# Low parts of three groups of weights made by VectorE in place of GpSimd, in a two-layer hybrid decoder

## The chip, the cores and the metric

The kernel runs on one core of a Trainium2 chip. The metric is the device time of one execution in microseconds (us), where less is better. The engines are named as in the profile: PE is TensorE's matmul stream and PEld its weight loads, DVE is VectorE, ACT is ScalarE, POOL is GpSimd, SP is SyncE, whose queue issues the kernel's DMA transfers.

## The reference

Two post-norm layers over x of 512 positions and 1024 features, all in float32. Each layer has a token mixer with three kinds of heads that read one combined projection of x, an output projection, a layer norm, a SwiGLU FFN of width 2816 and a second layer norm.

```python
proj = x @ w_in                                   # 1024 -> A 1152, B 768, C 416 columns
o_a = dilated_mixture(q, k, v, bias)              # A: 6 heads of 64, three (window, dilation) pairs
o_b = diff_attention(q1, q2, k1, k2, v, lam)      # B: 4 heads, two softmax maps each
o_b = rms_norm(o_b, subln_g) * (1 - lam_init)
c_q, c_kv, k_r = split(c_in, [256, 384])          # C: latents of 256 and 128, rotary key of 32
q  = rms_norm(c_q,  q_norm_g)  @ w_uq             # up-projection of the queries, 256 -> 6 x 96
kv = rms_norm(c_kv, kv_norm_g) @ w_ukv            # up-projection of keys and values, 128 -> 6 x 128
o_c = causal_attention(q_with_rope, k_with_rope, kv_values)
heads = concat([o_a, o_b, o_c])                   # 16 heads x 64 = 1024
h = layer_norm(ALPHA * x + heads @ w_o, ln1)      # output projection, 1024 x 1024
x = layer_norm(ALPHA * h + (silu(h @ w_gate) * (h @ w_up)) @ w_down, ln2)
```

## The kernel before

**Products in three parts.** Every float32 operand of a projection is split in two: a high part, which ACT writes as a rounded copy, and a low part, the operand minus its high part. A product is three matmuls (`mm3`, lines 210 to 212): high by high, high by low, low by high. So each chunk of weights goes through `split` (lines 199 to 205): ACT makes `whi` (line 201), and another engine makes `wlo` (line 202) from `raw` and `whi`, both in the core's own memory (SBUF).

**Chunks of weights.** `prep_one` brings one chunk of 128 rows and up to 1024 columns: SP issues the load into `raw` (two buffers, line 147), and `split` fills a pair of `whi` and `wlo` (five buffers of each). Chunks follow a fixed order over the whole kernel, and a step that needs some calls `chunks`, which prepares up to five ahead. Their names: `wva`, `wa` (A's values; queries and keys), `wvb`, `wb` (B's), `wc` (C's latents), `wu` (C's up-projections, three chunks of 768 columns a layer), `woa` and `wo` (output projection: four chunks of 768 columns for A's heads, five of 1024 for B's and C's), `wgu` and `wd` (FFN).

**Who makes the low part.** A table `ENG` names the engine for each group: "g" for GpSimd, "v" for VectorE. The norm factors of C (`q_norm_g`, `kv_norm_g`, in the tile `small`) are folded into the rows of `wu`. With GpSimd they are multiplied into `raw` by DVE first (line 159), and then the chunk is split like any other; with VectorE there is another path:

```python
        if scale is not None and eng is gp:
            v.tensor_scalar(raw[:, :w], raw[:, :w], scale, None, op0=ALU.mult)
            scale = None
        split(hi[:, :w], lo[:, :w], raw[:, :w], scale, eng)
...
            sc.activation(hi, src, AF.Copy, scale=scale)
            v.scalar_tensor_tensor(lo, src, scale, hi.bitcast(F32), op0=ALU.mult, op1=ALU.subtract)
```

**Steps of a layer's mixer.** `STEPS` lists them: values and queries of A and B, heads `AH`, `BH`, C's latents `CI`, their transposes `CT` (line 623, split into `x` by line 202), C's values `CV`, heads `CH`, norms of B `BN`, and shares of the output projection `W0` to `W5`, each of which adds a block of `heads @ w_o` into the residual (line 427) and gives PE work between the heads. `WC` is the rest of the output projection with the first layer norm. A softmax block (`softmax_block`) goes from PE's logits to DVE (line 289: bias and maximum; line 292: reciprocal), ACT (line 291: exponential) and POOL (line 299, for A and C: division by the sum). B's heads combine two maps: POOL scales one (line 566) and DVE adds the other (line 567). The maps are then transposed by PE (line 314), split into `pt` and `pu` by ACT and DVE, and multiplied by the values (line 536). C's queries are multiplied with the rotary table by DVE (line 656) and their low part is made by POOL (line 202, `qk<-m,qk`). `norm_b` spreads B's norm factors with a copy on DVE (line 582) and applies them (line 586).

**Order.** Each engine works through its own queue in the order in which the program was compiled. That order is set by a planner, which takes the ready instruction of the highest priority by a timeline with estimated costs; `PRIO` shifts single steps in it. So a change of the engine of an instruction can also change the order around it. SP's queue issues the loads of weights in line with the copies that stack queries and keys (line 525).

Of the kernel before, what the change touches and what calls it, by code (L numbers as in the profile page):

```python
# [49 lines left out]

ACTS = "qk qk m m qk qk m qk qk hd m hd qk hd qk qk e4 qk qk e4 qk qk".split()

ENG = {"wva": "g", "wa": "g", "wvb": "v", "wb": "g", "wc": "v", "wu": "g", "woa": "g", "wo": "g", "wgu0": "v",
       "wgu1": "v", "hA": "v", "hB": "g", "hC": "g", "qC": "g", "latq": "s", "latkv": "s"}

EARLY = 4
# [11 lines left out]
def hybrid_decoder(ctx: ExitStack, tc: tile.TileContext, I, out):  # L68
# [13 lines left out]
    def on(key):  # L82
        return {"v": v, "g": gp, "s": sc}[ENG.get(key, "v")]

# [865 lines left out]
```

## Time and profile before

| | us |
|---|---|
| median of 3 runs (lowest, highest) | 1212.33 (1210.52, 1213.17) |
| profiled execution, its own time | 1210.01 |
| its span, first to last instruction | 1208.2 |
| PE busy in the span | 1174.8 |
| DVE busy | 835.0 |
| ACT busy | 657.5 |
| POOL busy | 290.6 |

Busy times overlap, since the engines run side by side. An engine can be busy for longer than its instruction needs: a row's duration includes time in which the instruction had been started and waited for a port or a clock. Idle time of PE is what the other engines can still give back.

### The profile page before, as it was taken

To read this page: it belongs to the slowest core of one execution; us is meant where nothing else is said; L and a number is where in the kernel's file an instruction comes from. 1 tells how busy PE (TensorE), PEld (TensorE's weight loads), DVE (VectorE), ACT (ScalarE), POOL (GpSimd) and SP (SyncE) were. 2 spreads that over 40 slices of the span, in tenths; PEclk is the share of its full clock that TensorE was granted. 3 is DMA by queue.
4 is the path that set the end of the run, shared out by engine and by line. 5 is a ranking of instruction groups with operands and counts; after the bars stand their busy time and mean duration, and the time that the engine had idled before them with its cause. 6 is when DMAs were issued, how large, how long until landed. Compare 5 with 4: busy or idle time off the path is not lost.

```text
span 1208.2 us, 20278 instructions
## 1 busy us (share of the span) xinstructions
PE 1174.8 (97%) x7582; PEld 1073.2 (89%) x7582; DVE 835.0 (69%) x1655; ACT 657.5 (54%) x1290; POOL 290.6 (24%) x307
## 2 busy tenths in 40 slices
PE   9999999989999999999989999899999999999997
PEld 8889888889999999888888999787899999998885
DVE  5267788798888887443562677987988888864435
ACT  5466667666555555332443666775655565543322
POOL 1542576430000000000363435873200000000003
PEclk9999999999999999999999999999999999999999
DMA  7784321322333334333228544231123333344321
GB/s 263 201 243 136 116 75 46 97 69 88 106 106 105 102 99 136 119 114 95 80 88 232 149 131 124 82 106 35 55 91 108 110 105 94 105 140 132 96 70 70
DMA packets 50838, 136.41 MB, mean 113 GB/s; under 512 B 7731, under 2 KB 9267, under 8 KB 50739
## 3 DMA queue, kind: packets, MB, share of 16 engines
q1 hardware_dynamic: 50736, 135.10, 36.6%
q8 instruction: 60, 0.98, 0.3%
q14 instruction: 42, 0.32, 0.1%
HBM read 115.15 MB, written 2.10 MB: 97 GB/s over the span
## 4 chain that ended last, share of the span: by engine, by line
PE 55%; issue 29%; DVE 8%; ACT 3%; POOL 2%; DMA 2%; SPq 0%; POOLq 0%; ACTq 0%; DVEq 0%
PE psacc L210 10%; PE psacc L211 9%; PE psacc L212 9%; PE pss L210 4%; PE pss L212 4%; PE pss L211 4%; PE pspv L536 3%; PE pstp L314 2%; PE pss L286 2%; PE pstp L210 2%; PE pstp L211 2%; PE pstp L212 2%; DVE res L371 1%; POOL st L365 1%; DMA raw<-in_wva 1%
## 5 line engine op out<-in xcount | busy, mean ns | idle before, releaser
L201 ACT ACTIVATE whi<-raw 128x1024 fp32r<-128x1024 f32 (+2 forms) x150 | 153.4, 1025 | 130.0 <-PE pstp L212 26.2
L202 POOL TENSOR_TENSOR wlo<-raw,whi 128x1024 fp32r<-128x1024 f32 (+1 forms) x44 | 98.3, 2243 | 380.6 <-ACT whi L201 380.6
L202 DVE TENSOR_TENSOR wlo<-raw,whi 128x1024 fp32r<-128x1024 f32 (+1 forms) x106 | 129.1, 1221 | 47.8 <-ACT whi L201 47.7
L210 PE MATMUL psacc<-x,whi 128*128 128x256 f32 (+1 forms) x446 | 146.1, 333 | 2.3 <-ACT x L201 2.1
L202 DVE TENSOR_TENSOR wlo<-w,whi 128x1024 fp32r<-128x1024 f32 (+1 forms) x120 | 123.8, 1044 | 34.4 <-ACT whi L201 34.2
L211 PE MATMUL psacc<-x,whi 128*128 128x256 f32 (+1 forms) x446 | 147.0, 332 | 0.0
L212 PE MATMUL psacc<-x,wlo 128*128 128x256 f32 (+1 forms) x446 | 146.6, 331 | 0.0
L291 ACT ACTIVATE e<-e,sm 128x128 f32<-128x128 f32 (+3 forms) x160 | 89.4, 559 | 54.2 <-DVE sm L289 52.5
L201 ACT ACTIVATE whi<-w 128x1024 fp32r<-128x1024 f32 (+1 forms) x120 | 107.7, 909 | 6.3 <-DVE w L183 2.1
L210 PE MATMUL psacc<-whi,hd 128*128 128x512 f32 (+1 forms) x296 | 108.0, 367 | 2.0 <-DVE x L202 2.0
L211 PE MATMUL psacc<-wlo,hd 128*128 128x512 f32 (+1 forms) x296 | 106.6, 360 | 0.0
L212 PE MATMUL psacc<-whi,hd 128*128 128x512 f32 (+1 forms) x296 | 103.7, 360 | 0.0
L365 POOL TENSOR_TENSOR st<-st,mhalf 128x1 f32<-128x1 f32 x15 | 14.8, 988 | 349.6 <-DVE st L364 349.6
L210 PEld LDWEIGHTS psacc<-x,whi 128*128 128x128 f32 x446 | 84.0, 190 | 9.9 <-ACT x L201 2.6
L211 PEld LDWEIGHTS psacc<-x,whi 128*128 128x128 f32 x446 | 84.8, 190 | 7.3 <-DVE x L202 0.7
L210 PE MATMUL pss<-x,whi 128*128 128x256 f32 x320 | 91.2, 285 | 0.0
L212 PEld LDWEIGHTS psacc<-x,wlo 128*128 128x128 f32 x446 | 84.8, 190 | 6.9
L212 PE MATMUL pss<-x,wlo 128*128 128x256 f32 x320 | 90.6, 283 | 0.0
L212 PE MATMUL pss<-S,wlo 128*128 128x256 f32 x320 | 90.6, 283 | 0.0
L210 PE MATMUL pss<-S,whi 128*128 128x256 f32 x320 | 90.5, 283 | 0.0
L211 PE MATMUL pss<-S,whi 128*128 128x256 f32 x320 | 90.5, 283 | 0.0
L211 PE MATMUL pss<-x,whi 128*128 128x256 f32 x320 | 90.5, 283 | 0.0
(267 smaller groups left out, 3396.6 us busy)
## 6 DMA issues: line engine op xcount, KB each, us to landing
raw<-in_wgu SPq DMA_DIRECT2D x48, 512.0 KB, 3.6
raw<-in_wd SPq DMA_DIRECT2D x44, 512.0 KB, 3.5
w<-in_wgu SPq DMA_DIRECT2D x40, 512.0 KB, 4.4
qk<-qk SPq DMA_DIRECT2D x72, 128.0 KB, 4.5
qk<-qk SPq DMA_DIRECT2D x128, 64.0 KB, 2.0
raw<-in_wa SPq DMA_DIRECT2D x12, 512.0 KB, 3.6
bias<-in_bias SPq DMA_DIRECT2D x20, 256.0 KB, 4.4
raw<-in_wo SPq DMA_DIRECT2D x10, 512.0 KB, 3.6
```

The costliest lines, as they stand in the source:

```text
L201: sc.activation(hi, src, AF.Copy)
L202: eng.tensor_tensor(lo, src, hi.bitcast(F32), op=ALU.subtract)
L210: pe.matmul(o, ah, bh, start=first, stop=False, skip_group_check=parts)
L211: pe.matmul(o, ah, bl, start=False, stop=False, skip_group_check=parts)
L212: pe.matmul(o, al, bh, start=False, stop=last, skip_group_check=parts)
L286: pe.matmul(s[:, :w], q[:, i * P:(i + 1) * P], kn[:, :w], start=n == 0, stop=n == len(k) - 1)
L291: sc.activation(e, e, AF.Exp, bias=m, scale=-1.0, accum_out=den)
L314: pe.transpose(b[:, c:c + P], es[i][:, j * P:(j + 1) * P], ident)
L365: gp.tensor_tensor(rstd, var, mhalf[:, 0:1], op=ALU.pow)
L371: v.scalar_tensor_tensor(c, c, rstd, b[0], op0=ALU.mult, op1=ALU.add)
L536: pe.matmul(acc[:, j * P:], va, part, start=j + n == 0, stop=j + n == NTB)
```

## The change

Three entries of `ENG` change: the low parts of `wu`, `woa` and `wo` are made by VectorE. For `wu` this also takes the other path of `prep_one` and `split`: the multiplication of `raw` by the factors (line 159) is not issued, ACT multiplies while it writes the high part, and DVE makes the low part as `raw * factor - whi` in one instruction.

```diff
-ENG = {"wva": "g", "wa": "g", "wvb": "v", "wb": "g", "wc": "v", "wu": "g", "woa": "g", "wo": "g", "wgu0": "v",
+ENG = {"wva": "g", "wa": "g", "wvb": "v", "wb": "g", "wc": "v", "wu": "v", "woa": "v", "wo": "v", "wgu0": "v",
        "wgu1": "v", "hA": "v", "hB": "g", "hC": "g", "qC": "g", "latq": "s", "latkv": "s"}
```

## Rows read from the trace of the kernel before

**Rows 1.** The page, part 1: busy time, share of the span, instructions.

```profile
PE 1174.8 (97%) x7582; PEld 1073.2 (89%) x7582; DVE 835.0 (69%) x1655; ACT 657.5 (54%) x1290; POOL 290.6 (24%) x307
```

**Rows 2.** Windows: length, then busy PE, PEld, DVE, ACT, POOL, then PEclk, DMA.

```profile
140.00:232.00 92.00, 86.43 (x520) 76.03 (x519) 76.91 (x214) 65.50 (x152) 58.48 (x61) 0.94 0.29 89
750.00:832.00 82.00, 76.87 (x469) 66.34 (x469) 71.30 (x193) 61.64 (x142) 56.00 (x56) 1.00 0.27 84
```

**Rows 3.** Waits of PE in 140 to 232: total us, times, longest.

```profile
PE psacc L210 <- DVE x L202: 2.0, 1, 2.0
PE pstp L314 <- DVE e L567: 1.7, 1, 1.7
PE pss L286 <- DVE sm L289: 0.9, 1, 0.9
```

**Rows 4.** Waits of PE in 750 to 832.

```profile
PE pstp L314 <- DVE e L567: 2.1, 2, 1.2
PE pss L210 <- DVE sm L289: 1.0, 1, 1.0
```

**Rows 5.** Chain of work, 140 to 155: start, us, what.

```profile
141.02 3.57 DMA raw<-in_wu
...
144.62 0.62 DVE raw L159
...
146.38 2.04 DVE raw L159
...
149.07 0.58 PE psacc L210
```

**Rows 6.** Timeline of POOL, 136 to 150: start, us, instruction.

```profile
146.20 1.81 POOL L202 TENSOR_TENSOR wlo<-raw,whi 128x768 fp32r<-128x768 f32 x1 [0.15 <-ACT whi L201]
```

**Rows 7.** Windows, after two waits of PE and between them, columns alike.

```profile
147.90:154.70 6.80, 5.63 (x25) 5.53 (x26) 5.08 (x14) 3.77 (x7) 4.55 (x6) 0.50 0.33 116
155.00:161.80 6.80, 6.80 (x54) 6.77 (x54) 5.70 (x23) 5.09 (x13) 4.86 (x4) 1.00 0.52 145
182.00:185.40 3.40, 3.40 (x16) 3.10 (x14) 1.96 (x7) 2.99 (x8) 2.22 (x4) 0.50 0.31 122
```

**Rows 8.** Timeline, 177 to 185, two engines.

```profile
178.05 2.37 POOL L202 TENSOR_TENSOR wlo<-raw,whi 128x1024 fp32r<-128x1024 f32 x1
178.12 2.85 DVE L567 SCALAR_TENSOR_TENSOR e<-e,sm,e 128x512 f32<-128x512 f32 x1
```

**Rows 9.** Timeline of DVE, 752 to 800.

```profile
756.62 2.30 DVE L567 SCALAR_TENSOR_TENSOR e<-e,sm,e 128x512 f32<-128x512 f32 x1
...
774.25 0.43 DVE L582 COPY hd<-st 128x512 f32<-128x512 f32 x1
...
793.36 2.47 DVE L582 COPY hd<-st 128x512 f32<-128x512 f32 x1
```

**Rows 10.** Timeline of POOL, 750 to 806.

```profile
756.56 4.05 POOL L202 TENSOR_TENSOR wlo<-raw,whi 128x768 fp32r<-128x768 f32 x2
...
793.14 4.91 POOL L202 TENSOR_TENSOR wlo<-raw,whi 128x1024 fp32r<-128x1024 f32 x2
```

**Rows 11.** Groups of POOL by form: busy us, mean ns, idle before.

```profile
L202 POOL TENSOR_TENSOR wlo<-raw,whi 128x1024 fp32r<-128x1024 f32 x28 | 68.0, 2437 | 50.6 <-ACT whi L201 50.5
L202 POOL TENSOR_TENSOR wlo<-raw,whi 128x768 fp32r<-128x768 f32 x16 | 30.3, 1903 | 330.1 <-ACT whi L201 330.1
```

**Rows 12.** Groups of DVE by form.

```profile
L202 DVE TENSOR_TENSOR wlo<-raw,whi 128x832 fp32r<-128x832 f32 x8 | 8.2, 1025 | 1.3 <-ACT whi L201 1.3
...
L159 DVE TENSOR_SCALAR raw<-raw,small 128x768 f32<-128x768 f32 x6 | 5.3, 888 | 1.2 <-DMA raw<-in_wu 1.2
...
L586 DVE SCALAR_TENSOR_TENSOR hd<-hd,subg,pspv 128x512 f32<-128x512 f32 x4 | 3.0, 742 | 0.0
```

**Rows 13.** Line 202 on DVE, weights: ns min/median/max, first and last start.

```profile
L202 DVE TENSOR_TENSOR wlo<-raw,whi x106: 1007/1220/1898, 16.2 to 1174.3; 128x1024 fp32r<-128x1024 f32 x98, 128x832 fp32r<-128x832 f32 x8
```

**Rows 14.** Queue of SP, 118 to 160: issues merged.

```profile
132.21 8.69 SPq L525 DMA_DIRECT2D qk<-qk  x12
```

## Prediction

> **What bounds the kernel now.** I read the page first: PE is busy for 1174.8 of 1208.2 us [rows 1], so only some 33 us can be won by feeding it better. Then the waits of PE by stretch, to see whom it waits for. Wherever the three moved groups of weights are prepared, which is the second half of the mixer in each layer (about 140 to 232 us and 750 to 832 us), PE's releaser is DVE [rows 3, 4], through short instructions of the softmax, the splits and the combination of B's maps. These two stretches are the ones to study: PE is idle in them for 92.0 - 86.4 = 5.6 and 82.0 - 76.9 = 5.1 us, DVE is busy 84% and 87% of the time, POOL 64% and 68% [rows 2]. DVE is thus second in line, and at first sight the change gives it more to do. The next view speaks for the change: the timelines of DVE and POOL side by side. DVE's long instructions there are not long by nature. The combination of B's maps took 2.85 us at 178.12, beginning 0.07 us after a low part on POOL (178.05 to 180.42), and ended 0.55 us after it [rows 8]; an instruction of the same shape and operands takes 0.74 [rows 12]. The same happens at 756.62, 2.30 us beside two low parts [rows 9, 10]; the copy of B's norm factors takes 2.47 us beside two low parts and 0.43 elsewhere [rows 9, 10]; and the multiplication of C's factors took 2.04 us on the chain at 146.38, beside the low part that POOL had begun at 146.20, where the one before took 0.62 [rows 5, 6]. So a low part on POOL holds DVE up, and PE stands behind: 2.0 us at 149.07 [rows 3, 5], 1.7 us behind line 567 [rows 3], 1.2 us of the 2.1 in layer 2 [rows 4]. After the two longest waits PE also ran at half clock: PEclk is 0.50 (the 1.2 GHz level) from 147.9 to 154.7 and from 182.0 to 185.4, and 1.00 (2.4 GHz) between [rows 7].
>
> **What the change removes.** 24 instructions on POOL. Six low parts of wu and eight of woa at 1.90 us, and ten of wo at 2.44 [rows 11]: 14 x 1.90 + 10 x 2.44 = 51 us of POOL's 290.6 [rows 1]. It also removes six multiplications on DVE, 5.3 us with their stalls [rows 12].
>
> **What it adds.** 24 instructions on DVE. A low part of 1024 columns takes 1.22 us [rows 13], one of 832 columns 1.025 [rows 12], so one of 768 about 1.025 - 64 x (1.22 - 1.025) / 192 = 0.96. For wu the instruction also takes a factor for each row; the nearest row is the 512-column one of line 586, 0.742 us [rows 12], and at 1.025 / 832 = 1.23 ns a column, 768 come to 0.742 + 256 x 0.00123 = 1.06, with the 0.96 of the plain form as lower end. I take 1.0. In all 6 x 1.0 + 8 x 0.96 + 10 x 1.22 = 25.9 us, against 5.3 removed, and without the stalls seen above (2.11 + 1.56 of line 567, 2.04 of line 582): net about +15 us of DVE. The factors cost ACT nothing that I can bound above zero: it writes the same high parts, with a scale in the same instruction.
>
> **What a later order does to queues.** No load is added or moved in SP's list, but a raw buffer is now given back by DVE instead of POOL. In layer 1 the load of wu was issued at 141.02 and took 3.57 us to land [rows 5], because twelve copies of queries and keys occupied SP from 132.2 to 140.9 [rows 14]. If that stays, ACT must make the high part after the landing (it took about 1 us: from the end of the multiplication, 145.24, to the start of POOL's low part, 146.20 [rows 5, 6]), and the new instruction, if it stands at the head of DVE's queue, holds back from 144.6 to 145.6 and then works until 146.6, with the logits of B's head and the split of C's latents (line 202, `x`) behind it. A second chunk behind it would end near 147.6, and the split could begin there instead of at 148.42, the end of the second multiplication [rows 5]. So this place gains between 0.8 us (head of the queue) and 2.9 us (0.9 + 2.0 [rows 3], when it is elsewhere). I take 2.5, since the shorter occupation of the buffers lets the load go earlier.
>
> **The sum.** Gains on PE's side, if the stalls go:
> - 2.5 us at 145 to 149, as above, and the half clock behind it. There PE made 25 matmuls in 5.63 us (0.225 each) against 54 in 6.80 (0.126) at full clock [rows 7]; at that pace 25 would take 3.15, an estimate that neglects the mix of sizes: 2.5 us.
> - 1.7 us at 181 [rows 3], and 16 matmuls in 3.40 us [rows 7], which would take 2.0: 1.4 us.
> - in layer 2 1.2 us behind line 567, and 1.0 behind line 289 [rows 4], which came right after the stalled copy: 2.2 us.
>
> Together 10.3 us, at most about 10.7. Against this stands DVE. Taking those low parts that fell within the two stretches: layer 1 gets two of wu, two of woa and five of wo, 2.0 + 1.9 + 6.1 = 10.0 us, and loses 0.62 + 2.04 of multiplications and 2.11 of the stall: +5.2. Layer 2 gets two, one and five, 2.0 + 1.0 + 6.1 = 9.1 us, and loses 0.6, 1.56 and 2.04: +4.9. Together +10.1 us. DVE now idles there for 15.1 and 10.7 us [rows 2], 25.8 in all; if the stretches shrink by the whole 10.3, 15.5 are left, and the addition takes 10.1 / 15.5 = 0.65 of them. Nothing in the rows says which share of new work falls on the path that PE waits for. Its lower end is zero (all of it slips into idle time), its upper end all of it; I take the share of idle time that it uses up, 0.65, so 6.6 us are given back. Net: 10.3 - 6.6 = 3.7 us, and from the profiled 1210.0 this makes 1206.3. The median of the runs lies 2.3 us above the profiled execution, so I forecast 1208.5. Outside the two stretches, the first chunks of woa (two or three of 0.96 us in each layer) find DVE with room, and the FFN is untouched.
>
> **A rule against it.** A low part on DVE reads two operands in SBUF, and of 106 such low parts the longest took 1.90 us instead of 1.22 [rows 13]: they can be held up by POOL too, by up to 0.68. POOL after the change is busy in the two stretches for about 58.5 - 19.8 = 38.7 and 56.0 - 17.9 = 38.1 us, 42% and 46%; 17 low parts x 0.44 x 0.68 = 5.1 us of DVE at most, 3.3 on the path at the share above. The Trainium skill (SBUF — State Buffer, Who interferes with whom) states that a VectorE instruction with two inputs in SBUF and a GpSimd instruction that reads SBUF exclude each other for their whole length, whichever starts first going first. The stalls at 178.12 and 756.62 agree with it, in size too (2.85 us against the 2.37 of the low part). By that rule the new low parts would also hold up POOL's normalisations, so the change would exchange one exclusion for another.
>
> **Rivals.**
> - *DVE becomes the bound (slower).* Place: the heads of C in both layers, where low parts of 1.22 us stand in DVE's queue in front of the maxima (line 289), reciprocals and splits. For it: DVE is 84% and 87% busy already, and every wait of PE ends on it [rows 2 to 4]. Against it: POOL's queue gets shorter by 20 and 18 us, and POOL stands in the same softmax chains. Price: the gains of 10.3 are replaced by waits of the same length, and 0.65 of 10.1 us comes on top: 1212.3 + 6.6 = 1219; with half the gains kept, 1214. It decides once DVE would have to be over about 91% busy: (76.9 + 5.2 + 71.3 + 4.9) / 174 = 91% at the present lengths. The added work alone brings it there, which is why I take this rival seriously.
> - *The exclusion turns round (no change).* The 3.3 us above eat the net gain of 3.7: 1208.5 + 3.3 = 1211.8.
> - *All the gain stays.* The new work fits into DVE's idle time: 1212.3 - 10.3 = 1202.0, at best 1201.6.
>
> **Chances.** Net gain as summed, or more of it, 0.48 (of this, all the gain 0.10); the exclusion turned round or another balance within 0.2%, 0.21; DVE the bound, 0.31. About 0.2% (2.4 us) is what a measurement of this kernel can tell from no change. The likeliest alone has 1202 to 1210. The range for 8 in 10 goes from 1201, all gains, to 1217, between the two prices of the slower rival.
>
> **What the profile after would show.** Right: line 159 is gone; line 202 has 20 instructions on POOL under `wlo`; lines 567 and 582 have no duration above 2 us beside a low part (beside `qk<-m,qk` some of 1.5 remain); PEclk stays at 1.00 from 147 to 185; POOL is busy for about 240 us, DVE for about 850; PE's waits in the two stretches sum to under 6 us. Wrong: waits of PE that end on lines 289, 202 or 567 of DVE with a low part of `wu`, `woa` or `wo` just before them in DVE's queue; DVE above 93% in the stretches; low parts on DVE of 1.6 us and more; a new half-clock stretch after such a wait. A planner's order that differs in steps far from the change (queries, B's heads) would also make it wrong; the trace before cannot tell of that.

## The result: half a per cent slower, and the profile after

| us | before | after |
|---|---|---|
| median of 9 runs each (lowest, highest) | 1211.82 (1209.46, 1213.17) | 1218.65 (1212.66, 1219.90) |
| ratio, 95% interval | | 1.0053 [1.0039, 1.0067] |
| profiled execution, its span | 1210.01, 1208.2 | 1219.52, 1217.7 |

The change costs about 6.4 us by the ratio. The forecast was 1208.5, faster by 3.7 us; the range ended at 1217.

Busy times of the whole span, part 1 of the page, beside [rows 1]:

```profile
PE 1181.4 (97%) x7582; PEld 1078.4 (89%) x7582; DVE 845.8 (69%) x1673; ACT 658.4 (54%) x1290; POOL 245.6 (20%) x283
```

POOL lost 45 us and 24 instructions, DVE gained 10.8 us. The two stretches, beside [rows 2]:

```profile
140.00:232.00 92.00, 87.08 (x538) 76.45 (x537) 82.12 (x230) 65.56 (x157) 42.50 (x53) 0.98 0.30 92
750.00:832.00 82.00, 76.94 (x461) 68.04 (x461) 74.77 (x197) 58.45 (x135) 34.63 (x43) 0.96 0.29 96
```

DVE went from 84% to 89% and from 87% to 91%; that it was not more is the point to which the experiments come back. Line 159 is gone, and what was moved costs what was forecast (groups of DVE by form, then of POOL, beside [rows 11, 12]):

```profile
L567 DVE SCALAR_TENSOR_TENSOR e<-e,sm,e 128x512 f32<-128x512 f32 x8 | 8.3, 1035 | 1.3 <-POOL e L566 1.3
...
L202 DVE TENSOR_TENSOR wlo<-raw,whi 128x768 fp32r<-128x768 f32 x8 | 7.9, 990 | 0.4 <-ACT whi L201 0.3
...
L205 DVE SCALAR_TENSOR_TENSOR wlo<-raw,small,whi 128x768 fp32r<-128x768 f32 x6 | 6.1, 1014 | 0.8 <-ACT whi L204 0.8
```

```profile
L202 POOL TENSOR_TENSOR wlo<-raw,whi 128x1024 fp32r<-128x1024 f32 x18 | 43.4, 2421 | 47.7 <-ACT whi L201 47.6
...
L202 POOL TENSOR_TENSOR wlo<-raw,whi 128x768 fp32r<-128x768 f32 x2 | 3.7, 1845 | 320.6 <-ACT whi L201 320.6
```

PE's waits in 140 to 232, beside [rows 3], and then in 750 to 832, beside [rows 4]:

```profile
PE pstp L314 <- DVE e L567: 2.5, 1, 2.5
PE pstp L314 <- DVE pu L202: 0.6, 1, 0.6
```

```profile
PE pss L210 <- DVE sm L289: 1.8, 2, 1.5
PE psacc L210 <- DVE x L202: 1.1, 1, 1.1
PE pstp L314 <- DVE e L567: 0.8, 1, 0.8
PE pspv L536 <- DVE hd L586: 0.7, 1, 0.7
```

The wait of 2.0 us on the split of C's latents is gone in layer 1, as forecast. The wait behind line 567 has grown from 1.7 to 2.5, though line 567 is no longer held up for 2.85 us by a low part of POOL. In layer 2 the waits have become more. PE's idle time in the two windows is still 4.9 and 5.1 us.

Two timelines show the new exclusions. First DVE (two rows) and POOL (one row) at 178:

```profile
178.62 1.24 DVE L202 TENSOR_TENSOR wlo<-raw,whi 128x1024 fp32r<-128x1024 f32 x1
180.46 1.74 DVE L567 SCALAR_TENSOR_TENSOR e<-e,sm,e 128x512 f32<-128x512 f32 x1 [0.59 <-POOL e L566]
...
178.62 1.81 POOL L566 TENSOR_SCALAR e<-e,sm,neglam 128x512 f32<-128x512 f32 x1 [0.60 <-DVE sm L292]
```

The low part, now on DVE, and POOL's scaling of B's second map begin together; the low part takes its usual 1.24 us, the scaling 1.81 where the same shape took 0.77 at 782.40 in this run. Line 567, which needs it, waits 0.59 us, and PE behind it. Then at 785, DVE and POOL:

```profile
785.39 1.82 DVE L202 TENSOR_TENSOR wlo<-raw,whi 128x1024 fp32r<-128x1024 f32 x1
...
783.14 2.99 POOL L202 TENSOR_TENSOR qk<-m,qk 128x512 fp32r<-128x512 f32 x2
```

Here POOL was first, and the low part took 1.82 us. The Trainium skill (SBUF — State Buffer, Who interferes with whom) says that the one that starts first goes first and the other stands for its whole length; the case at 785 agrees in kind, with 0.6 us added to the low part.

One part of the profiled difference comes before the first moved instruction. Up to 113 us the queues of both kernels are alike, yet this execution was 4.1 us late at 98 us, behind a wait for a copy of queries into place (timeline of PE):

```profile
83.66 0.58 PE L210 MATMUL psacc<-whi,x 128*128 128x256 f32 x1 [3.65 <-DVE qk L205]
```

In the profile of before this wait was 0.2 us; in other executions of the same two kernels it was 1.58 us (before, again) and 2.02 us (after, again). So the profiles are compared below by stretch, and the verdicts rest on medians.

### The profile page after: what moved, and what is told of

Its sections match the earlier page's. It is cut to its first block, busy times and chain, and to the rows that moved or that the text cites. A ratio compares the mean times of both kernels' runs of the same rounds, so it can differ in the third digit from the quotient of the medians.

```text
span 1217.7 us, 20264 instructions
## 1 busy us (share of the span) xinstructions
PE 1181.4 (97%) x7582; PEld 1078.4 (89%) x7582; DVE 845.8 (69%) x1673; ACT 658.4 (54%) x1290; POOL 245.6 (20%) x283
## 4 chain that ended last, share of the span: by engine, by line
PE 54%; issue 29%; DVE 9%; DMA 3%; POOL 2%; ACT 2%; POOLq 0%; ACTq 0%; DVEq 0%
PE psacc L210 9%; PE psacc L211 9%; PE psacc L212 9%; PE pss L210 4%; PE pss L212 4%; PE pss L211 4%; PE pspv L536 3%; PE pstp L314 2%; PE pstp L210 2%; PE pss L286 2%; PE pstp L211 2%; PE pstp L212 2%; DVE wlo L202 1%; DVE res L371 1%; DMA qk<-qk 1%
## 5 line engine op out<-in xcount | busy, mean ns | idle before, releaser
L201 ACT ACTIVATE whi<-raw 128x1024 fp32r<-128x1024 f32 (+2 forms) x144 | 148.4, 1032 | 128.0 <-PE pstp L212 27.3
L202 DVE TENSOR_TENSOR wlo<-raw,whi 128x1024 fp32r<-128x1024 f32 (+2 forms) x124 | 150.1, 1213 | 47.4 <-ACT whi L201 47.2
L202 POOL TENSOR_TENSOR wlo<-raw,whi 128x1024 fp32r<-128x1024 f32 (+1 forms) x20 | 47.1, 2363 | 368.2 <-ACT whi L201 368.2
L289 DVE CUSTOM_DVE_ANT_0 e<-pss,bias 128x128 f32<-128x128 f32 (+3 forms) x160 | 76.1, 476 | 15.9 <-PE pss L286 12.2
```

The source lines that it names most:

```text
L201: sc.activation(hi, src, AF.Copy)
L202: eng.tensor_tensor(lo, src, hi.bitcast(F32), op=ALU.subtract)
L289: v.tensor_tensor_reduce(out=e, in0=s[:, :w], in1=bias[:, S - w:], op0=ALU.add, op1=ALU.min, scale=-1.0, scalar=-NEG, accum_out=m)
```

## The experiments

Theories, under the letters of the texts on record where they have one there. **L (load):** in the second halves of the mixers, what DVE is given comes out on PE's path nearly whole. **P (planned order):** moving 24 instructions makes the planner lay out the work anew, and the loss is in that layout. **C (chain):** only the wait for the low part itself, or the exclusion of two readers, costs; work that nobody waits for does not. At first also **A**, that the low parts of `wu` gain and those of the output projection lose, and its rival **O**, that any change of an engine disturbs the order by as much. In the first two texts C and D mean something else: that the early wait near 83 us belongs to the changed program (C), or comes and goes with the execution (D). Ratios are to before on the same chip, with 95% intervals.

**1 and 2. Both kernels again** (no edit).

> The kernel before, unchanged, timed and profiled once more. Up to about 115 us the queues of all engines are alike in the kernels before and after, yet the profile of after has a wait of PE of 3.6 us near 83 us that the profile of before has not (0.2 us there, 1.7 us a little later). Theory D (that wait is a matter of when the copies of queries and keys land, and comes and goes from one execution to the next): ratio 1.000, and single times spread over some 4 us; the wait near 83 us can be there or not. Theory C (it belongs to the changed program): no wait above 2 us near 83 us here.

> The changed kernel, unchanged, timed and profiled once more. Theory C (the wait near 83 us belongs to the changed program): the wait of 3 to 4 us is there again, and the ratio stays at 1.005 to 1.006. Theory D: it may be gone, and then the span is some 4 us shorter, about 1213.5; the ratio over many runs then holds a mean of both. In both, the waits of the second half of layer 2 stay: about 5 us are lost between 740 and 835 us.

Measured: before 0.9991 [0.9974, 1.0008]; after 1216.84 us, 1.0048 [1.0031, 1.0065]. The loss is confirmed, and D held: the wait near 83 us was 1.58 and 2.02 us here, and between the same matmuls of layer 2 (740 to 832 us) the second profile of the change lost 4.2 us. The second profile of before held a surprise. Both long waits of layer 1 are there again:

```profile
PE psacc L210 <- DVE x L202: 2.0, 1, 2.0
PE pstp L314 <- DVE e L567: 1.7, 1, 1.7
```

but the clock behind them is full (windows from each wait on, PEclk after the counts; compare the 0.50 in [rows 7]):

```profile
149.00:152.40 3.40, 3.40 (x29) 3.36 (x30) 3.40 (x11) 2.44 (x7) 3.25 (x3) 1.00 0.37 115
181.00:184.40 3.40, 3.40 (x28) 3.21 (x27) 3.20 (x8) 2.38 (x7) 1.88 (x2) 1.00 0.06 20
```

So the half clock behind these two waits was a matter of that execution, and two terms of the sum rested on it.

**3 and 4. One half of the change each.**

```diff
-       "wu": "g", "woa": "g", "wo": "g"
+       "wu": "v", "woa": "g", "wo": "g"      # 3
+       "wu": "g", "woa": "v", "wo": "v"      # 4
```

> Only the low parts of C's up-projection go to VectorE (with the factors in the same instruction); woa and wo stay on GpSimd. Theory A (the loss comes from low parts of woa and wo in VectorE's queue between the heads of C, while wu alone removes the multiplication that a low part on GpSimd held up): a gain of 3 to 5 us near 145 to 155 us in layer 1 stays, nothing is lost behind it, ratio 0.996 to 0.999. Rival O (any change of an engine disturbs the planned order by as much): a loss of 2 us or more, ratio above 1.002.

> Only the low parts of the output projection (woa and wo, 18 chunks) go to VectorE; wu stays on GpSimd with its multiplication on VectorE. Theory A: all of the loss and more, 5 to 9 us, ratio 1.004 to 1.008, since the gain near 150 us is not there. Rival O: between 0.999 and 1.004, with no relation to the parts.

Measured: `wu` alone 1.0044 [1.0027, 1.0060], `woa` and `wo` alone 1.0076 [1.0052, 1.0100]. Theory A fell with the first of the two (0.996 to 0.999 expected), O with the second (0.999 to 1.004). And the halves come to 1.2% together, the whole to 0.5%: something other than these instructions differs among the kernels, and that can be their order.

**5. The change in layer 1 alone.**

```diff
         eng = on(...)
+        if name in ("wu", "woa", "wo") and l == 0:
+            eng = v
```

> The change in layer 1 alone; layer 2 keeps GpSimd's low parts. Theory L: layer 1's second half as in the change (0 to 3 us later than before by 237 us), layer 2's second half as in before (0, within 1.5 us), together 1.001 to 1.003 (1212 to 1215). Theory P: the planner's layout of layer 2 differs as well, so layer 2 need not be as in before: its second half comes out anywhere from 2 us earlier to 10 us later although none of its instructions has changed, and the total 1.000 to 1.008.

Measured: 1.0017 [1.0001, 1.0033], inside the forecast of L. Layer 2's second half ran as in before, with the same waits (1.29 and 0.82 us behind 567, 0.98 behind 289). So most of the loss belongs to layer 2.

**6 to 8. Engines and order taken apart.** The kernel is traced twice in one program. The first trace, with one choice of engines, is planned; its order is then imposed on the second, with another choice, by edges that bind the issue order of each engine and are not meant to add a wait. The six multiplications of line 159, which only one of the two traces has, are left to the planner.

```python
for n in ranks:                       # the planned order of the first trace
    i = traced[n]                     # the same instruction in the second
    if i.engine in last:
        tc.add_manual_dep(i, last[i.engine], mybir.DependencyInfo(
            mybir.DependencyClass.NoSync, mybir.DependencyReason.DATA), reason="order")
    last[i.engine] = i.name
```

> The kernel before, with its own planned order written down and then imposed on every engine as order-only edges: the control for the two kernels that mix engines and orders. All theories: same as before, ratio 0.999 to 1.001 (1209.5 to 1213). If it is outside that, the edges themselves cost something and the other two are to be read against this kernel.

> The low parts are made by VectorE as in the change, but every engine keeps the order that was planned for the kernel before (each low part stands in VectorE's queue at the place in the global order where GpSimd's stood). Theory L (the load: VectorE's net 10 us in the two stretches stand on the path, wherever they are put): 1.004 to 1.006, as the change (1215 to 1218). Theory P (the planned order: the planner lays all the work out anew when the costs move, and the loss is in that layout): 0.998 to 1.001 (1208 to 1212), the waits of 2.0 and 1.7 us at 149 and 179 us gone, and no new one above 1.5 us in the two stretches. Half of each would be 1.002 to 1.003.

> The low parts stay on GpSimd as in the kernel before (VectorE keeps its separate multiplication for the wu slabs), but every engine has the order that was planned for the change. Theory L: no load is moved, so 0.999 to 1.002 (1209 to 1214). Theory P: slower like the change or more, 1.004 to 1.009 (1215 to 1221), since an order planned for other costs is kept and the exclusion between GpSimd and VectorE is back as well. A value of 1.004 or more together with 1.004 or more for the change in the order of before would say that both cost by themselves.

Measured: the control 1.0012 [0.9990, 1.0034]; the change in the order of before 1.0037 [1.0018, 1.0056]; the engines of before in the order of the change 1.0181 [1.0152, 1.0210]. The control's interval includes no change, so a cost of the edges is not seen. P's forecast for the second (up to 1.001) fell: most of the loss is there without any new order, just under L's 1.004. L's forecast for the third (up to 1.002) fell too, and P's (up to 1.009) was too small: an order planned for other engines costs a lot, 22 us. So both matter, and the new order is in part the planner's answer to the new load.

**9 to 11. The parts, and extra load, in the order of before.** `wu` alone; `woa` and `wo` alone; and the whole change with a spare read behind each of the 24 low parts, which nobody waits for (shortened; it is bound right behind its low part):

```diff
         split(hi[:, :w], lo[:, :w], raw[:, :w], scale, eng)
+        v.tensor_reduce(spare, hi[:, :w].bitcast(F32), op=ALU.max, axis=mybir.AxisListType.X)
```

> Only the low parts of wu by VectorE, every engine in the order planned for before. Theory L: VectorE's net load in the two stretches is about 4 us less 0.6 + 2.0 + 0.6 of multiplications, so about +1, and the stall at 150 us goes: 0.998 to 1.000 (1207.5 to 1210), where the same change under its own planned order gave 1.0044. If it is 1.003 or more, the low parts of wu cost by their place and not by their load.

> Only the low parts of woa and wo by VectorE, every engine in the order planned for before. Theory L: nearly all of the net load of the change (1.9 + 6.1 and 1.0 + 6.1 us in the two stretches), and the stall at 150 us stays: 1.003 to 1.007 (1213.5 to 1218), no less than the whole change in that order. If it is within 0.999 to 1.002, the loss is not in the output projection's low parts, and the sum of the two parts is not the whole even in a fixed order.

> The change in the order planned for before, and behind each of the 24 moved low parts one instruction more in VectorE's queue: a maximum over the row of the high part, written to a spare column that nobody reads (about 0.8 to 1.1 us each by its size, 19 to 26 us in all, estimated from the low parts). Theory L (load: what VectorE is given in these stretches comes out on the path at a share of about 0.65 or more): 12 to 20 us slower than the change in the order of before, 1.013 to 1.02 in ratio to before. Theory C (what counts is the chain: the matmuls wait for the low part itself, or the stalls come from two readers of SBUF; work that nobody waits for slips into idle time): within 3 us of the change in the order of before, 1.003 to 1.006.

> The change in the order planned for before once more, as the partner of the three others on the same chip: 1.002 to 1.0055, as its first run (1.0037). All theories alike.

Measured: `wu` alone 0.9994 [0.9979, 1.0010]; `woa` and `wo` alone 1.0049 [1.0032, 1.0065]; the whole, second run, 1214.19 us, 1.0030 [1.0016, 1.0045]; with spare reads 1239.4 us, 1.0239 [1.0217, 1.0260]. C fell. Their row in the groups by line:

```profile
L165 DVE TENSOR_REDUCE spare<-whi 128x1 f32<-128x768 f32 (+1 forms) x24 | 25.3, 1054 | 0.0
```

25.3 us of DVE made the kernel 1239.4 - 1214.2 = 25.2 us slower, to within some 3 us by the two intervals. So reads that nobody waits for cost about their whole length. L had expected 12 to 20: even its share was too small. `wu` alone is level in a fixed order, where it had cost 0.44% in its own: there the planner's order was the loss.

**12. The same reads in the FFN.** Engines and order of before, 24 spare reads behind low parts of `wd` (shortened alike).

```diff
+        if ENG.get("spare") and name == "wd" and 4 <= i < 16:
+            v.tensor_reduce(spare, hi[:, :w].bitcast(F32), op=ALU.max, axis=mybir.AxisListType.X)
```

> The engines and the order of before, and 24 spare reads in VectorE's queue as in the earlier run, but behind low parts of wd in the FFNs, where VectorE is busy 40% to 60% of the time. If the slope of 1 belongs to the stretches in which VectorE is nearly full: 0.998 to 1.002 (1208 to 1213), within 3 us of the control. If VectorE's work costs its length wherever it stands: 1.015 to 1.021 (1228 to 1236).

Measured: 0.9997 [0.9983, 1.0010]. The groups by line, and the window of the reads in layer 1:

```profile
L165 DVE TENSOR_REDUCE spare<-whi 128x1 f32<-128x1024 f32 x24 | 29.1, 1213 | 0.0
```

```profile
493.00:545.00 52.00, 52.00 (x231) 43.09 (x230) 35.79 (x38) 18.59 (x25) 0.00 (x0) 1.00 0.40 122
```

29.1 us more for DVE, and no change: DVE is busy 35.8 of 52 us there (23.7 in the same window of before) and PE never waits. The slope of 1 belongs to the two stretches.

**13 and 14. Own order against order of before, side by side.**

> The change once more, in its own planned order. Load and order together: 1.004 to 1.006. If only the load costs, it comes out like its partner in the order of before.

> The change in the order planned for before, third run, partner of the one above. If the order costs on top of the load: 1.002 to 1.004 and 0.001 to 0.003 under the partner. If only the load costs: within 0.001 of the partner.

Measured: 1217.62 us, 1.0049 [1.0031, 1.0066], and 1214.87 us, 1.0031 [1.0016, 1.0046]. The three runs of the change in its own order gave 1.0053, 1.0048, 1.0049, the three in the order of before 1.0037, 1.0030, 1.0031. The distance of 0.0017 (0.0050 - 0.0033 in the mean, about 2 us) has the same sign against each, but the intervals of single runs overlap. Its place is not shown. In layer 1 all three profiles of the change have a wait of 2.45 to 2.47 us behind line 567, where the three in the order of before have one of 0.7 behind 567 and one of 1.1 behind 289. Counted as in the table below, the own order lost 2.1, 0.1 and 1.3 us in layer 1 and 5.0, 4.2 and 4.0 in layer 2: in the mean 1.2 more and 0.6 less than the order of before.

**Matmul for matmul.** In a fixed order PE's n-th matmul is the same in every kernel. How much later than in the control it starts, grown over each stretch (matmuls 739 to 1277, and 4534 to 5084, which the control starts at 140 and 232, 740 and 832 us), in us:

| order of before | layer 1 | layer 2 |
|---|---|---|
| before, first profile | +3.1 | 0.0 |
| before, second profile | -0.8 | 0.0 |
| `wu` moved | -1.6 | +0.7 |
| `woa`, `wo` moved | 0.0 | +5.1 |
| the change, three runs | -0.6, -0.9, +1.4 | +5.2, +5.0, +4.9 |
| the change and spare reads | +11.9 | +15.2 |
| spare reads in the FFN | -1.3 | +0.3 |

Layer 2 loses 5 us three times over, and with the output projection alone. Layer 1 comes out even. (Before's first profile is late in layer 1 by its 10.2 us of half clock.) Against the second run of the change the spare reads add 11.9 + 0.9 = 12.8 us in layer 1 and 15.2 - 5.0 = 10.2 us in layer 2. In each, 9 reads (9.8 us) start between the two matmuls and 2 more up to 3.5 us before: 23.0 us for 19.6 to 23.4 of reads.

One place shows how. Timeline of DVE in the control:

```profile
774.61 0.43 DVE L582 COPY hd<-st 128x512 f32<-128x512 f32 x1
...
775.63 1.53 DVE L567 SCALAR_TENSOR_TENSOR e<-e,sm,e 128x384 f32<-128x384 f32 x1
...
777.42 0.73 DVE L586 SCALAR_TENSOR_TENSOR hd<-hd,subg,pspv 128x512 f32<-128x512 f32 x1
778.08 1.52 DVE L567 SCALAR_TENSOR_TENSOR e<-e,sm,e 128x512 f32<-128x512 f32 x1
```

and with the change, the same queue (the second run in the order of before):

```profile
771.82 0.43 DVE L582 COPY hd<-st 128x512 f32<-128x512 f32 x1
...
772.83 1.55 DVE L567 SCALAR_TENSOR_TENSOR e<-e,sm,e 128x384 f32<-128x384 f32 x1
...
774.64 1.45 DVE L202 TENSOR_TENSOR wlo<-raw,whi 128x1024 fp32r<-128x1024 f32 x1
776.02 0.73 DVE L586 SCALAR_TENSOR_TENSOR hd<-hd,subg,pspv 128x512 f32<-128x512 f32 x1
776.67 1.09 DVE L567 SCALAR_TENSOR_TENSOR e<-e,sm,e 128x512 f32<-128x512 f32 x1
```

From the copy to the last row's start are 778.08 - 774.61 = 3.47 us without the low part and 776.67 - 771.82 = 4.85 with it: 1.38 more, the low part's 1.45 almost whole, since DVE has no idle time between these rows. To the last row's end 5.94 - 4.99 = 0.95 us are left, since that row takes 1.09 in place of 1.52. PE's wait behind that instruction of line 567 grew from 0.80 us (at 779.66) to 1.97 (at 777.82). After this wait, and after one of 1.0 us at 798.25, PE ran at half clock:

```profile
778.50:781.90 3.40, 3.40 (x16) 3.40 (x17) 3.10 (x9) 3.35 (x8) 3.40 (x5) 0.50 0.09 36
799.00:802.40 3.40, 3.40 (x11) 3.21 (x12) 2.32 (x9) 2.39 (x8) 2.30 (x3) 0.50 0.12 46
```

The windows between the same matmuls, layer 1 and layer 2, in the control, then with the change in that order (second run), then with spare reads:

```profile
140.06:232.06 92.00, 86.49 (x541) 76.13 (x539) 79.34 (x221) 67.38 (x157) 60.89 (x65) 0.98 0.29 91
740.03:832.18 92.15, 87.03 (x551) 76.42 (x551) 81.09 (x231) 69.24 (x165) 61.22 (x65) 1.00 0.30 91
```

```profile
138.54:229.61 91.07, 85.48 (x540) 74.60 (x538) 82.45 (x228) 67.34 (x158) 42.68 (x55) 1.00 0.29 91
736.10:833.23 97.13, 90.34 (x551) 79.41 (x551) 85.52 (x237) 69.70 (x165) 41.79 (x55) 0.96 0.27 87
```

```profile
141.51:245.41 103.90, 89.96 (x540) 76.01 (x538) 94.45 (x243) 67.84 (x158) 42.26 (x55) 0.98 0.25 80
754.93:862.27 107.34, 94.32 (x551) 82.73 (x551) 95.87 (x248) 69.52 (x165) 41.50 (x55) 0.92 0.24 79
```

DVE's idle time is the length less its busy time. In layer 2 it is 11.1, 11.6 and 11.5 us: 4.4 us more DVE work make 5.0 us of time, and another 10.4 make 10.2. DVE was as full before as it gets in this stretch, at 88%. In layer 1 there was some room: the idle time falls from 12.7 us (11.4 in before's second profile) to 8.6, and 3.1 us more DVE work cost no time; the spare reads find it at 9.4, and 12.0 us more make 12.8.

Half clock could be another cause in layer 2: the three runs of the change in this order, and `woa` and `wo` alone, have 6.8 us of it there, the control none. But the second profile of the change in its own order lost 4.2 us between these matmuls at full clock:

```profile
739.37:835.74 96.37, 89.15 (x553) 76.64 (x553) 86.14 (x237) 69.80 (x165) 41.69 (x55) 1.00 0.28 88
```

The kernel with spare reads has more half clock too, 17.1 us in layer 2, but only 3.4 us in layer 1, where the reads cost no less.

## Why the prediction was wrong

The rival "DVE becomes the bound" (1214 to 1219) came nearest, and in layer 2 what it describes is what happened. That the median of 1218.65 is its upper number is in part luck: it let the gains turn into waits in both layers, layer 1 came out even, and about 2 us belong to the planner's order. Its condition, DVE above 91% busy, was too high: 88% was full in layer 2. By layers, in the order of before (less is faster):

| us | forecast | measured |
|---|---|---|
| layer 1 | 0.65 x 5.2 - 8.1 = -4.7 | -0.8 (mean of three runs, against that of the control and two profiles of before) |
| layer 2 | 0.65 x 4.9 - 2.2 = +1.0 | +5.0 |
| the planner's own order | not in the sum | about +2 |

Point by point:

- **What bounds the kernel.** That PE waits for DVE in these stretches was right. The step that failed is the price of the added DVE work: DVE's idle 15.1 and 10.7 us [rows 2] were read as room. In layer 2 none of it was; in layer 1 some 3 us were, and part of the 15.1 came from the half clock of that execution.
- **The share of 0.65 (failed).** Measured: 25.2 us of time for 25.3 of spare work, 5.0 for 4.4 in layer 2. The net addition itself was a little smaller than summed, 3.1 and 4.4 us instead of 5.2 and 4.9. The idle time is in gaps in which DVE waits for its own inputs, mostly from ACT and PE; work put behind a low part does not fall into them in layer 2 but delays what comes next.
- **Layer 2's gains of 2.2 us (failed).** They were counted twice: the removed stalls (1.56 and 2.04 us) already lower DVE's net 4.9, and where DVE's work sets the time, that is all that they can give (read from the windows above, not tried by a run of its own). The wait of 1.25 us at 759 in the control became 0.38, with 0.59 right after it. The one of 1.0 behind line 289 stayed (0.98 in the control, 1.00), although the copy of line 582 before it fell from 2.47 to 0.42 us: two low parts (1.22 and 1.84) stand there now. And a wait of 0.80 became 1.97.
- **Half clock, 2.5 and 1.4 us (mis-sized).** Behind these two waits stood 10.2 us of half clock in the first profile of before, none in the second and 3.4 in the control. In the mean, 4.5 us, the two terms are worth 3.9 x 4.5 / 10.2 = 1.7 instead of 3.9.
- **145 to 149 us (right in kind).** With `wu` on DVE the 2.0 us wait is gone in the change's own order, and 0.49 to 0.75 in the order of before. By the matmul that the control starts at 165 us, the three runs had grown 1.9 to 2.1 us ahead of it (before's second profile 0.9); 1.2 to 3.5 of this was lost again by 232. With the order held, `wu` alone is 0.8 us quicker in layer 1 than before's second profile (-1.6 against -0.8), less than runs of one kernel differ there.
- **1.7 us at 181 (failed).** The low parts of POOL no longer hold line 567 up, as forecast, but in the change's own order a low part in DVE's own queue, with POOL's scaling held up by it, puts PE's wait back: 2.45 us at 182. In the order of before there are two of 0.7 and 1.1 in its place.
- **The exclusion turned round (seen).** Low parts of 1.45 to 1.85 us instead of 1.22, once 2.38, and a scaling of 1.81. The two in layer 2 in the order of before come to 0.9 us; how much of this reaches PE was not tried. The prediction's 0.74 for an unhindered line 567 is right (0.75 at 723.45 in before), though line 586, from which it was taken, reads one operand from `pspv` in place of a second `e`.
- **The planned order.** The prediction named it as a thing that could not be told from the trace of before. It adds about 2 us to the whole change, 0.5% to `wu` alone, 22 us when kept for the wrong engines.

The sum again (its last step, 1206.3 + 2.3, gives 1208.6, where 1208.5 was written): with a share of 1 and the half clock at its mean, 10.3 - 2.2 of gains less 10.1 makes the change 2.0 us slower. In the order of before it was 0.33% or 4.0 us slower. Without layer 2's 2.2 the sum gives 4.2. This agreement is of the whole only: in layer 1 both the gains and the added work were smaller than summed, and the half clock behind the new waits (about 0.5 us grown from 780 to 790 and 1.1 from 800 to 810, in the second run) is not in it.

Of the signs named beforehand, these came right: line 159 gone, 20 low parts left on POOL, 246 us of POOL, 846 of DVE, no line 567 above 2 us. These did not: PEclk at 1.00 from 147 to 185 (0.50 from 182.1 for 3.4 us) and PE's waits under 6 us together (10.0 us idle in the two windows). These wrong ones came: low parts in front of lines 567, 289 and 202, one of 1.82 us, and new half-clock stretches after such waits. DVE above 93% did not come; it was full below that.

What stays open: which instruction of the planner's own order costs the 2 us, and why layer 1 had some room where layer 2 had none. No version that beats both kernels came up; the nearest, `wu` alone in the order of before, is level with before.

## What to carry to other kernels

An engine that is second in the list of busy times can be full where it matters, here at 88%: in a stretch in which nearly every wait of the busiest engine ends on it, count new work at its whole length unless a run shows room, and count a stall that goes away once, on that engine or as a wait, not as both. Spare work that nobody waits for, put into its queue there and elsewhere in the same order, measures that slope in two runs. Where a planner orders the queues, hold the order fixed to tell the price of an instruction from that of the new layout; and take no term from a half clock that only one profile shows.

## What the runs showed of the hardware

- The same waits of 2.0 and 1.7 us, in the same program, were followed by 6.8 and 3.4 us at the 1.2 GHz level in one execution, by full clock in another, and by 3.4 us after the first of them alone in a third (the control, with the same queues).
- A wait on line 205 behind identical queues, for a copy landing before 84 us, was between 0.2 and 3.65 us in five profiles of the two kernels, with nothing changed before it in the program.
- Where a VectorE low part and a POOL scaling began at the same time (178.62, and likewise in the two other profiles of the change), only POOL's took longer: 1.80 to 1.81 us, the low part 1.24.
- In layer 2's stretch, in the order of before, VectorE's idle time stayed at 11.1 to 11.6 us while its work between the same matmuls went from 81.1 to 85.5 and 95.9 us.
